# Gate and up products of a pair of experts, issued alternately for the one and the other expert

## Chip, cores and metric

The kernel runs on one core of a Trainium2 chip. The metric is device time in microseconds (us) of one execution, the median of several runs. Lower is better.

## What is computed

Two transformer blocks on 256 tokens of width 1024, all in fp32. The second ends with a mixture of experts: 32 experts in 4 groups, two of them per token, each expert a gated feed-forward layer of hidden width 512. Cut to what matters here (the routing gives `expert`, `weights` and the blocks of tokens per expert):

```python
def hier_moe(h, w_rg, b_rg, w_re, b_re, w_gate, w_up, w_down):
    ...
    def run_block(args):
        e, tok, w = args
        xb = xt[tok]
        hid = jax.nn.silu(xb @ w_gate[e]) * (xb @ w_up[e])
        return (hid @ w_down[e]) * w[:, None].astype(xb.dtype)
    ...
x = x + hier_moe(rmsnorm_2(x, g_moe[l]), ...)
return rmsnorm_2(x, g_final)
```

An expert's weights are 1024x512 (gate), 1024x512 (up) and 512x1024 (down) fp32 numbers, 2 MiB each, so all 32 experts have 192 MiB that must come from HBM.

## The kernel before

Everything up to the experts (both mixers, the first block's feed-forward layer, the cross attention) comes first and takes about 640 us; the change does not touch it. Then `moe` (lines 2045 to 2247) takes the experts two at a time. A pair `p` has experts `2p` and `2p+1`, here called `j = 0` and `j = 1`. Each expert has 64 places for tokens (`CAP`), so the two together fill 128 partitions: `H[0]` is partitions 0 to 63 and `H[1]` is 64 to 127. A product of one expert uses 64 columns of TensorE's array and writes 64 partitions of a PSUM bank; the other expert uses the other 64.

One turn of the loop over pairs issues, in this order:

- `gather` (every second turn, for two pairs): the tokens of the next experts, as columns, into `xe` (32 matmuls of 128x256).
- `hid_T`: four transposes of pair `p`'s hidden values (`sg`), copied to `hdT` by ScalarE.
- `gate_up(p+1)` (line 2097): gate and up products of the next pair. `k` runs over 8 slices of the width 1024, `c` is 0 for gate and 1 for up; `g[c]` is one PSUM bank for each. That is 8 x 2 x 2 = 32 products of 64x512. In the trace each fp32 product is two MATMUL instructions, so 64. After the first eight products (the first unit of weights of each expert, `k` 0 and 1) it calls `between`: `combine` (8 matmuls that add the pair before to the result) and `slots_T` (2 transposes). Then come the other 24 products.
- `down(p)` (line 2121): 4 slices x 2 halves `c` x 2 experts = 16 products of 64x512 (32 instructions). Here `j` already runs innermost.

After the last pair come `combine`, the final norm and the output (`norm_first`, `norm_out`).

The weights come in units of 1 MiB. A unit of `gate_up` holds the gate and the up rows of one expert for two values of `k` and is fetched as two transfers of 512 KiB; a unit of `down` is one transfer of 1 MiB (the last two units come as halves). `Experts.order` (line 349) lists them: 8 units for gate and up of pair 0, then for each pair the 8 units of the next pair's gate and up followed by the 4 units of its own down, the two experts' units alternating. All transfers are issued on SyncE's queue (SP), into 22 buffers in turn (`slots`: 4, then 5, then 13); a transfer waits until TensorE's last read of the unit that was in the buffer 22 units earlier. So TensorE has a store of up to 22 units, nearly two pairs, ahead of it.

TensorE issues its instructions in program order of `mm`, and the change moves only those of `gate_up`:

Of the kernel before, what the change touches and what calls it, by code (L numbers as in the profile page):

```python
# [421 lines left out]
class K:  # L422
# [1622 lines left out]
    def moe(self, A):  # L2045
# [51 lines left out]
        def gate_up(n, j0, ws_, between=None):  # L2097

            g = [self.bank() for _ in range(2)]
            for k, j, c in [(2 * q + i, j, c) for q in range(4) for j in range(n) for i in range(2) for c in range(2)]:  # L2100
                if between and (k, j, c) == (2, 0, 0):
                    between()
                self.mm(g[c][H[j]], xe[:, k, j0 + j], ws_(j, k // 2)[:, c, k % 2], k == 0, k == 7)
            sg = self.sg
            R = slice(0, n * CAP)
            nc.scalar.activation(sg[R], g[0][R], AF.Silu)
            V.tensor_tensor(sg[R], g[1][R], sg[R], op=ALU.mult)
            return sg
# [76 lines left out]
        quad = lambda p: rk[:, :, 2 * p:min(2 * p + 4, NE)]  # L2185
        gather(2, self.oh, [x])
        hd = gate_up(2, 0, unit(0))
        for t in range(2):
            nc.scalar.activation(xh[t], x[t], AF.Copy, scale=self.r[:, t:t + 1])
# [7 lines left out]
        for p in range(NP):  # L2197
            n = min(4, NE - 2 * (p + 1))
            if p % 2 == 0 and n:
                gather(n, oh, [xh, xl])  # L2200
            hdT = hid_T(2, hd)
            pw = one_hot(2, col(rk, p), col(W32, p))
            if p % 2 and p + 2 < NP:
                oh = hot(quad(p + 2), min(4, NE - 2 * (p + 2)))

            def between():
                nonlocal pT
                if p:
                    combine(pT)
                pT = slots_T(2, pw)  # L2210
            if n:
                hd = gate_up(2, 2 * (p % 2), unit(p + 1), between)
                X.load(12 * p + 16 + NR)
            else:
                final_gain()
                between()
                keep(NLAST)
            down(2, hdT, unit(p))
            X.load(12 * p + 20 + NR)
# [5 lines left out]
        with tc.If(most > CAP):  # L2225
            with tc.For_i(0, NE, 1) as e:
                one = bass.ds(e, 1)
                rke = A.tile([128, 2, 2], F32, name="rke")
                V.tensor_copy(rke[:, 0, :, None], rk[:, :, one])
                V.tensor_copy(rke[:, 1, :, None], W32[:, :, one])  # L2230
                wu = [X.fetch(spare[q], one, q) for q in range(6)]
                rk_, w_ = (lambda t, j: rke[:, 0, t:t + 1]), (lambda t, j: rke[:, 1, t:t + 1])
                for _ in range(1, T // CAP):
                    V.tensor_scalar(rke[:, 0], rke[:, 0], -float(CAP), None, op0=ALU.add)
                    gather(1, hot(rke[:, 0, :, None], 1), [xh, xl])
                    pT = slots_T(1, one_hot(1, rk_, w_))
                    down(1, hid_T(1, gate_up(1, 0, lambda j, q: wu[q])), lambda j, q: wu[q])
                    for c in range(2):
                        for t in range(2):
                            b = self.bank()  # L2240
                            for i in range(2):
                                self.mm(b, pT[H[0], t * 128:(t + 1) * 128], ys[c][i][H[0]], i == 0, i == 1)
                            sum_ = spare[7 + c][:, t * 512:(t + 1) * 512]
                            nc.scalar.activation(sum_, acc[t][c], AF.Copy)
                            V.tensor_tensor(acc[t][c], b, sum_, op=ALU.add)
            norm_first()
            norm_out()
# [27 lines left out]
```

## Time and profile before

| | |
|---|---|
| median of 3 runs | 1132.79 us (1130.45 to 1132.81) |
| profiled execution | 1131.38 us |
| its span, first to last instruction | 1129.6 us |
| TensorE matmul busy (PE) | 1107.8 us, 98% |
| TensorE weight load busy (PEld) | 784.5 us, 69% |
| VectorE, ScalarE, GpSimd busy | 45%, 34%, 5% |
| chain of work that ended last | 93% on PE |
| read from HBM | 297.83 MB |

The span begins at 0 and ends with the last instruction; all times in the rows below are from its start. "Busy" of PE is the time in which at least one matmul was under way, so two matmuls side by side in the two halves of the array count once. A view of stretches gives for each engine the busy time and, in brackets, the instructions; then the granted clock of TensorE as a share of 2.4 GHz, the share of time in which the DMA engines were busy, and GB/s.

### The profile page before, as it was taken

Reading aid. Unit: us, or ns where it says so; the run is one execution under the profiler, and the core shown is the slowest. Engines: PE = TensorE matmul, PEld = TensorE weight load, DVE = VectorE, ACT = ScalarE, POOL = GpSimd, SP = SyncE. Lnnn points to the kernel's source line nnn. Section 1 sums busy time; section 2 is a strip of 40 time slices with the busy share of each in tenths; the row PEclk is TensorE's granted clock in tenths of the full one; section 3 lists DMA queues with packets and bytes.
Section 4 is the critical chain, followed back from the end, with each engine's and each line's share of the span. In section 5 each row is a group of like instructions: output and inputs, shape, how many; then the busy total and the mean of one; then the engine's idle time right before and its main releaser. Section 6 shows DMA issues by size and latency. Waiting matters only on the chain.

```text
span 1129.6 us, 16831 instructions
## 1 busy us (share of the span) xinstructions
PE 1107.8 (98%) x6850; PEld 784.5 (69%) x6850; DVE 504.1 (45%) x917; ACT 381.2 (34%) x678; POOL 57.3 (5%) x85
## 2 busy tenths in 40 slices
PE   9999999999999999999999989999999999999996
PEld 8989788999999887989988644444444445444453
DVE  5777756656556576665666321212121212111112
ACT  6553556544344475565454210000000000000103
POOL 0153011000000010100000000000000000000000
PEclk9999999999999999999999999999999999999999
DMA  8454216674664544545498689999999999999931
GB/s 299 136 165 133 76 38 199 254 246 167 197 189 162 172 150 152 179 126 180 161 359 335 243 337 407 411 413 411 413 412 413 413 413 414 413 413 413 415 156 40
DMA packets 105950, 300.06 MB, mean 266 GB/s; under 512 B 6999, under 2 KB 35980, under 8 KB 97932
## 3 DMA queue, kind: packets, MB, share of 16 engines
q1 hardware_dynamic: 104700, 295.23, 69.6%
q0 software_dynamic: 1024, 3.17, 1.0%
q8 instruction: 56, 0.92, 0.3%
q10 hardware_dynamic: 144, 0.52, 0.1%
q14 instruction: 26, 0.21, 0.1%
HBM read 297.83 MB, written 1.07 MB: 265 GB/s over the span
## 4 chain that ended last, share of the span: by engine, by line
PE 93%; DVE 3%; ACT 2%; issue 1%; DMA 0%; POOL 0%; SPq 0%; ACTq 0%; DVEq 0%
PE bank L249 93%; ACT junk L249 1%; DVE cy L249 0%; DMA x<-in_x 0%; DVE junk L249 0%; DVE xTl L249 0%; ACT wh L249 0%; DVE x L249 0%; DVE xl L249 0%; ACT xTh L249 0%; DVE wm L249 0%; ACT sg L249 0%; DVE dp L249 0%; POOL nr L249 0%; DVE smz L249 0%
## 5 line engine op out<-in xcount | busy, mean ns | idle before, releaser
L249 PE MATMUL bank<-wm,xe 128*64 128x512 f32 x1024 | 285.1, 598 | 0.0
L249 DVE TENSOR_TENSOR wl<-wr,wh 128x1024 fp32r<-128x1024 f32 (+1 forms) x175 | 211.0, 1222 | 134.2 <-ACT wh L249 130.8
L249 PE MATMUL bank<-xTh,wh 128*128 128x256 f32 x768 | 223.1, 291 | 0.0
L249 ACT ACTIVATE wh<-wr 128x1024 fp32r<-128x1024 f32 (+1 forms) x175 | 180.1, 1050 | 118.2 <-PE bank L249 104.6
L249 PE MATMUL bank<-xTl,wh 128*128 128x256 f32 x768 | 217.3, 283 | 0.8 <-DVE xTl L249 0.8
L249 PE MATMUL bank<-xTh,wl 128*128 128x256 f32 x768 | 217.1, 283 | 0.2 <-DVE wl L249 0.2
L249 PEld LDWEIGHTS bank<-wm,xe 128*64 128x64 f32 x1024 | 101.0, 136 | 160.3 <-issue 157.1
L249 PEld LDWEIGHTS bank<-xTh,wh 128*128 128x128 f32 x768 | 147.0, 191 | 4.6 <-issue 2.4
L249 PEld LDWEIGHTS bank<-xTl,wh 128*128 128x128 f32 x768 | 147.1, 192 | 2.3 <-DVE xTl L249 1.2
L249 PEld LDWEIGHTS bank<-xTh,wl 128*128 128x128 f32 x768 | 147.0, 191 | 0.4 <-DVE wl L249 0.4
L249 PE MATMUL bank<-wm,hdT 128*64 128x512 f32 x512 | 128.7, 595 | 0.0
L249 ACT ACTIVATE sg<-bank 128x512 f32<-128x512 f32 x20 | 11.9, 597 | 295.3 <-PE bank L249 295.2
L249 DVE TENSOR_TENSOR sg<-bank,sg 128x512 f32<-128x512 f32 x16 | 11.1, 691 | 191.7 <-PE bank L249 191.7
L249 PEld LDWEIGHTS bank<-wm,hdT 128*64 128x64 f32 x512 | 46.5, 137 | 65.9 <-issue 60.7
L249 DVE SCALAR_TENSOR_TENSOR ys<-bank,ws,ys 128x512 fp32r<-128x512 f32 x32 | 24.0, 751 | 98.8 <-ACT ys L249 96.9
L249 ACT ACTIVATE ys<-bank,ws 128x512 fp32r<-128x512 f32 x32 | 22.0, 688 | 106.1 <-PE bank L249 106.1
L249 DVE TENSOR_SCALAR pwT<-bank 128x256 fp32r<-128x256 f32 x16 | 6.8, 424 | 90.1 <-PE bank L249 90.1
L249 POOL TENSOR_TENSOR nr<-nr,mhalf 128x2 f32<-128x2 f32 (+1 forms) x9 | 6.0, 673 | 713.0 <-DVE nr L249 712.9
L249 PE MATMUL bank<-wl,fhh 128*128 128x512 f32 x88 | 35.2, 400 | 0.0
L249 PE MATMUL bank<-wh,fhh 128*128 128x512 f32 x88 | 34.8, 395 | 0.0
L249 PEld LDWEIGHTS bank<-ys,pwT 128*128 128x128 f32 x128 | 22.8, 188 | 17.2 <-issue 11.4
L249 PE MATMUL bank<-ys,pwT 128*128 128x512 f32 x128 | 34.3, 408 | 0.3 <-DVE ys L249 0.3
(386 smaller groups left out, 1477.0 us busy)
## 6 DMA issues: line engine op xcount, KB each, us to landing
wm<-in_w_exp_gate SPq DMA_DIRECT2D x128, 512.0 KB, 10.2
wm<-in_w_exp_up SPq DMA_DIRECT2D x128, 512.0 KB, 10.2
wm<-in_w_exp_down SPq DMA_DIRECT2D x62, 1024.0 KB, 12.6
wr<-in_w_in SPq DMA_DIRECT2D x33, 1024.0 KB, 5.2
wr<-in_w_gate_up SPq DMA_DIRECT2D x22, 1024.0 KB, 5.7
wr<-in_w_down SPq DMA_DIRECT2D x11, 1024.0 KB, 5.1
wr<-in_w_out SPq DMA_DIRECT2D x8, 1024.0 KB, 5.1
wr<-in_w_ckv SPq DMA_DIRECT2D x4, 1024.0 KB, 6.3
```

The lines of the kernel that those rows point to most:

```text
L249: r = f(*args, **kw)
```

## The change

The list of products in `gate_up` is written in another order. Before, `q` (the unit) is outermost, then the expert `j`, then the two slices of the unit, then gate and up. After, the slice `k` is outermost, then gate and up, and the expert innermost. The test for `between` is rewritten for the new order and fires at the same place, after the first eight products.

```diff
         def gate_up(n, j0, ws_, between=None):
 
             g = [self.bank() for _ in range(2)]
-            for k, j, c in [(2 * q + i, j, c) for q in range(4) for j in range(n) for i in range(2) for c in range(2)]:
-                if between and (k, j, c) == (2, 0, 0):
+            for k, c, j in [(k, c, j) for k in range(8) for c in range(2) for j in range(n)]:
+                if between and (k, c, j) == (2, 0, 0):
                     between()
                 self.mm(g[c][H[j]], xe[:, k, j0 + j], ws_(j, k // 2)[:, c, k % 2], k == 0, k == 7)
```

No instruction is added or removed, and the orders of VectorE, ScalarE, GpSimd and SP stay as they are. On TensorE the first place is the first eight products of a `gate_up`, ahead of `between`. A row is one product: the bank it writes (`bank0_74` gate, `bank2_76` up), the weights' buffer (`wm2_6220` of the first expert, `wm3_6221` of the second) and the DMA counters it waits for. Before:

```order
L249 MATMUL bank0_74<-wm2_6220,xe_69 64x512 [waits DMAHW5_49]
L249 MATMUL bank2_76<-wm2_6220,xe_69 64x512 [waits DMAHW6_49,DVE_49]
L249 MATMUL bank0_74<-wm2_6220,xe_69 64x512
L249 MATMUL bank2_76<-wm2_6220,xe_69 64x512
L249 MATMUL bank0_74<-wm3_6221,xe_69 64x512 [waits DMAHW7_49]
L249 MATMUL bank2_76<-wm3_6221,xe_69 64x512 [waits DMAHW0_49]
L249 MATMUL bank0_74<-wm3_6221,xe_69 64x512
L249 MATMUL bank2_76<-wm3_6221,xe_69 64x512
```

After, at the same place on TensorE:

```order
L249 MATMUL bank0_74<-wm2_6220,xe_69 64x512 [waits DMAHW5_49]
L249 MATMUL bank0_74<-wm3_6221,xe_69 64x512 [waits DMAHW7_49]
L249 MATMUL bank2_76<-wm2_6220,xe_69 64x512 [waits DMAHW6_49,DVE_49]
L249 MATMUL bank2_76<-wm3_6221,xe_69 64x512 [waits DMAHW0_49]
L249 MATMUL bank0_74<-wm2_6220,xe_69 64x512
L249 MATMUL bank0_74<-wm3_6221,xe_69 64x512
L249 MATMUL bank2_76<-wm2_6220,xe_69 64x512
L249 MATMUL bank2_76<-wm3_6221,xe_69 64x512
```

Before, four products of the first expert are followed by four of the second; after, every other product is of the other expert, and the second expert's unit is waited for at the second product instead of the fifth.

The second place is the end of a `gate_up` on TensorE, where `down` (the rows that read `hdT_70`) follows without a break. Before:

```order
L249 MATMUL bank7_81<-wm12_6230,xe_69 64x512
L249 MATMUL bank3_77<-wm8_6226,xe_69 64x512 [waits DMAHW7_49]
L249 MATMUL bank7_81<-wm8_6226,xe_69 64x512 [waits DMAHW0_49]
L249 MATMUL bank3_77<-wm8_6226,xe_69 64x512
L249 MATMUL bank7_81<-wm8_6226,xe_69 64x512
L249 MATMUL bank2_76<-wm9_6227,hdT_70 64x512 [waits DMAHW1_49,Activation_49]
L249 MATMUL bank2_76<-wm6_6224,hdT_70 64x512 [waits DMAHW2_49]
L249 MATMUL bank3_77<-wm9_6227,hdT_70 64x512 [waits Activation_49]
```

After, at the same place on TensorE:

```order
L249 MATMUL bank7_81<-wm8_6226,xe_69 64x512 [waits DMAHW0_49]
L249 MATMUL bank3_77<-wm12_6230,xe_69 64x512
L249 MATMUL bank3_77<-wm8_6226,xe_69 64x512
L249 MATMUL bank7_81<-wm12_6230,xe_69 64x512
L249 MATMUL bank7_81<-wm8_6226,xe_69 64x512
L249 MATMUL bank2_76<-wm9_6227,hdT_70 64x512 [waits DMAHW1_49,Activation_49]
L249 MATMUL bank2_76<-wm6_6224,hdT_70 64x512 [waits DMAHW2_49]
L249 MATMUL bank3_77<-wm9_6227,hdT_70 64x512 [waits Activation_49]
```

Before, the four products ahead of `down` all belong to the second expert (`wm8_6226`); after, they alternate. `down` keeps its order, and its third product writes the bank of gate (`bank3_77`), so it waits until ScalarE has read that bank.

## Rows read from the trace of the kernel before

**Rows 1.** Page, parts 1 and 2: PE's busy time; DMA share and GB/s in 40 slices.
```profile
PE 1107.8 (98%) x6850; PEld 784.5 (69%) x6850; DVE 504.1 (45%) x917; ACT 381.2 (34%) x678; POOL 57.3 (5%) x85
...
DMA  8454216674664544545498689999999999999931
GB/s 299 136 165 133 76 38 199 254 246 167 197 189 162 172 150 152 179 126 180 161 359 335 243 337 407 411 413 411 413 412 413 413 413 414 413 413 413 415 156 40
```

**Rows 2.** Timeline of PE, one pair: start us, us, engine line op out<-in xcount.
```profile
927.96 5.42 PE L249 MATMUL bank<-wm,xe 128*64 128x512 f32 x16
933.31 2.13 PE L249 MATMUL bank<-ys,pwT 128*128 128x512 f32 x8
...
935.58 11.23 PE L249 MATMUL bank<-wm,xe 128*64 128x512 f32 x45
946.22 0.64 PE L249 MATMUL bank<-wm,hdT 128*64 128x512 f32 x1
946.65 0.59 PE L249 MATMUL bank<-wm,xe 128*64 128x512 f32 x1
...
947.93 7.04 PE L249 MATMUL bank<-wm,hdT 128*64 128x512 f32 x30
```

**Rows 3.** Timeline of PEld (weight loads), the same pair's gate-and-up and down.
```profile
928.87 0.14 PEld L249 LDWEIGHTS bank<-wm,xe 128*64 128x64 f32 x1 [0.29 <-issue]
...
929.73 0.19 PEld L249 LDWEIGHTS bank<-wm,xe 128*64 128x64 f32 x3 [0.29 <-issue]
...
948.37 0.18 PEld L249 LDWEIGHTS bank<-wm,hdT 128*64 128x64 f32 x2 [0.25 <-issue]
...
952.23 0.18 PEld L249 LDWEIGHTS bank<-wm,hdT 128*64 128x64 f32 x2 [0.25 <-issue]
```

**Rows 4.** Busy time by stretch: first gate-and-up; last pair to the end.
```profile
640.56:656.63 16.07, 16.06 (x65) 6.03 (x64) 0.69 (x1) 0.83 (x2) 0.00 (x0) 1.00 0.76 281
1104.54:1129.60 25.06, 14.87 (x73) 8.01 (x72) 7.77 (x16) 7.95 (x16) 1.12 (x2) 0.89 0.13 45
```

**Rows 5.** Busy time by stretch: the weights' stream, its steady part and its end.
```profile
681.00:1080.00 399.00, 399.00 (x1710) 180.56 (x1708) 74.31 (x157) 35.45 (x56) 0.00 (x0) 1.00 1.02 413
...
1084.00:1086.00 2.00, 2.00 (x9) 1.16 (x8) 0.66 (x2) 0.00 (x0) 0.00 (x0) 1.00 0.21 84
1086.00:1090.00 4.00, 4.00 (x17) 1.57 (x17) 0.09 (x1) 0.00 (x0) 0.00 (x0) 1.00 0.00 0
```

**Rows 6.** Page, part 6: sizes of the experts' transfers.
```profile
wm<-in_w_exp_gate SPq DMA_DIRECT2D x128, 512.0 KB, 10.2
...
wm<-in_w_exp_down SPq DMA_DIRECT2D x62, 1024.0 KB, 12.6
```

**Rows 7.** Timeline of PE: the last pair's transposes and down products.
```profile
1104.54 0.74 PE L249 MATMUL bank<-cst,sg 128*128 128x128 f32 x4
...
1109.94 7.09 PE L249 MATMUL bank<-wm,hdT 128*64 128x512 f32 x32
```

**Rows 8.** Busy time by stretch: the stream's stall after the first pair.
```profile
666.00:671.00 5.00, 5.00 (x16) 1.64 (x16) 1.11 (x5) 0.60 (x1) 0.00 (x0) 1.00 0.11 20
671.00:676.00 5.00, 5.00 (x19) 1.91 (x20) 0.76 (x2) 0.00 (x0) 0.00 (x0) 1.00 0.95 390
676.00:681.00 5.00, 5.00 (x26) 2.04 (x24) 0.00 (x0) 0.00 (x0) 0.00 (x0) 1.00 0.97 353
```

**Rows 9.** Timeline of SP: its issues around that stall.
```profile
654.88 16.81 SPq L249 DMA_DIRECT2D wm<-in_w_exp_down  x4
674.45 0.33 SPq L249 DMA_DIRECT2D wm<-in_w_exp_gate  x1
```

**Rows 10.** Busy time by stretch: TensorE short of work, and the granted clock.
```profile
390.20:393.70 3.50, 1.91 (x17) 1.68 (x17) 1.57 (x4) 1.90 (x8) 0.00 (x0) 1.00 0.48 186
...
656.00:661.00 5.00, 2.03 (x7) 1.05 (x6) 3.68 (x4) 2.46 (x3) 0.00 (x0) 0.89 1.03 412
661.00:666.00 5.00, 5.00 (x34) 4.88 (x33) 2.54 (x4) 0.00 (x0) 0.00 (x0) 0.76 0.98 407
```

## The prediction

> **What bounds the kernel now.** I read the page first. PE is busy 98% of the span, and in slices 25 to 37 the DMA engines are busy too, 9 tenths, moving 407 to 415 GB/s [rows 1]. Two things are near their limit in the experts' stage, so the next question is which of them ends last. The view by stretches answers it: from 681 to 1080 us the weights' stream runs at 413 GB/s with a busy share of 1.02, between 1084 and 1086 it falls to 84, and after 1086 it moves nothing [rows 5]. I take 1085.7 for its last landing. TensorE starts the last pair's transposes only at 1104.54 and its down products end at 1109.94 + 7.09 = 1117.03 [rows 7]. So today TensorE ends some 31 us behind the stream, and the stream itself has almost no room left.
>
> How TensorE spends its time is seen in the timeline of one pair. The two experts use two halves of the array, and the halves can work side by side. In the down products, where the experts alternate, two weight loads start together every (952.23 - 948.37) / 9 = 0.429 us [rows 3]: one instruction of each half per 0.429 us, which I call a slot. The last pair's 32 down instructions are 16 slots, 6.86 us, and take 7.09 [rows 7], so a run costs 0.23 us beside its slots. In gate and up, single loads mark stretches in which one half works alone (928.87), and loads by twos and threes those in which both do (929.73) [rows 3].
>
> A rule of the Trainium skill bears on this. The timeline first: a down product starts at 946.22, ahead of a gate-or-up product at 946.65 that stands before it in the program [rows 2], so one half does run ahead of the other. "TensorE: Matmul & The Clock Gate", Part 3 ("What overlaps and what doesn't"), says that matmuls start and end strictly in program order. By that, the 64 instructions of a gate-and-up would now take nearly 64 slots, 27 us, and the order would be worth some 13 us a pair on TensorE; the rows give (933.31 - 927.96) + (946.22 - 935.58) = 16.0 us [rows 2], so the trace disagrees, and the sum goes by the rows: most of the pairing exists already, and only the ends of each run, where one half is done before the other, are to be had.
>
> **The change, part by part.** Nothing is added or removed; the moves are on TensorE alone.
> - *First eight products*, 16 instructions ahead of the combine: 5.35 us now (927.96 to 933.31) [rows 2]. Alternating they are 8 slots + 0.23 = 3.66. Saved: 1.7.
> - *The other 24 and the 32 down instructions behind them*: from 935.58 to 947.93 + 7.04 = 954.97, 19.39 us [rows 2]. Alternating throughout they are 48 + 32 = 80 instructions, 40 slots + 0.23 = 17.39. Saved: 2.0.
> - *First pair's gate-and-up*, alone: 64 instructions in 16.07 us [rows 4]; 32 slots + 0.23 = 13.96. Saved: 2.1.
> - Sum on TensorE: 15 pairs x 3.7 + 2.1 = 57.6 us.
> - *Waits*: the second expert's unit is now needed at the second product, not the fifth. While the stream is ahead this costs nothing. Behind TensorE's queue then stand that pair's combine and down products. Once the stream limits, a step of two units needs both units in either order, and 16 instructions follow the later one: no difference worth a number. Down's third product waits for ScalarE's read of gate's bank; in the new order gate's last products end two slots ahead of up's, and up's last products and down's first two cover that read. Were a slot lost there in each pair, it would take 15 x 0.429 = 6.4 us of TensorE's gain, and not yet any of the kernel's, as comes below.
>
> That sum cannot all arrive, because the stream is the next to be late. A pair's weights are 16 x 512 KiB + 4 x 1 MiB [rows 6] = 12.58 MB, at 413 GB/s 30.5 us. TensorE, busy without a break from about 661, takes (1104.54 - 661) / 15 = 29.6 us a pair [rows 7, 10], and would take 25.9. It uses up its lag, then waits for landings. Unhindered it would start the last pair's transposes at 1104.54 - 57.6 = 1046.9; the stream does not allow it. The last pair's four down units (4.19 MB, 10.2 us) are the last to land, so the units of the pair before it are complete at 1085.7 - 10.2 = 1075.5. On them follow 16 instructions, 3.66 us, and the last pair's transposes at 1079.2: 25.3 us earlier than now. From there to the end 25.06 us stay as they are [rows 4]. The last down products would start 5.4 us later, at 1084.6, and need the last half unit only for their last quarter, so the stream's very end is covered.
>
> The second term is when the stream starts to run full. It stalls from 666 to 681 us, moving 20, 390 and 353 GB/s; against 413 that is 4.8 + 0.3 + 0.7 = 5.8 us lost [rows 8]. SP waits there for TensorE to free buffers: four issues run from 654.88 to 671.4, the next comes at 674.45 [rows 9]. In the changed kernel the products it waits for come 2.1 us earlier and their run is 1.7 shorter, 3.8 together. But the first expert's buffer, free today after its block alone, is then free only with the other's, so the first waiting issue gains just 2.1. Everything behind it gains 3.8. I take 3.5, near the larger end since all but one issue have it; the bounds are 0 (the stream ramps up as slowly as now) and 5.8 (the whole stall goes).
>
> **Sum.** 25.3 + 3.5 = 28.8 us. Against the profiled execution: 1131.38 - 28.8 = 1102.6; the median of the runs shown is 1.4 higher, so **1104.0 us** on its scale. Bounds: 1132.8 - 25.3 = 1107.5 above and 1131.4 - 31.1 = 1100.3 below. TensorE gains 57.6 and the kernel half of it; half the gain per pair (28.8 / 15 = 1.9) would be enough.
>
> **Rivals.**
> 1. *The halves do not pair further*, and the order does nothing: 1132.8. Against it: the down products have this very order, two instructions a slot [rows 3]. A part of the pairing gives something between; 1 us a pair would give 1132.8 - 15 - 2 = 1116.
> 2. *The clock falls in the waits, and the kernel gets slower.* TensorE would wait 28.8 us in all, 30.5 - 25.9 = 4.6 a pair, so over the last six pairs. When it had 2.03 us of work in 5, from 656 to 661, the granted clock went to its lower level: 0.89 in that stretch, 0.76 in the next [rows 10]. At half clock a pair takes 51.8 us, 21.3 more than the stream. More than 28.8 / 21.3 = 1.4 pairs' worth of it and the kernel is slower than before; all six would give about 1104 + 128 = 1232. Against it: from 390 to 394 us TensorE worked 1.91 of 3.50 us and the clock stayed at 1.00 [rows 10], and the waits to come are shorter: a step of two units takes the stream 2.10 MB / 413 = 5.1 us and TensorE 3.66, a wait of 1.4.
> 3. *Weight loads come out of cover.* In rows 3 a load of 0.14 us starts with each instruction inside a 0.429 us slot, hidden. If two loads a slot stood outside, a slot would be 0.71, and the 48 slots of a pair 13.4 us longer than forecast, 9.7 longer than now; with the first pair's 6.9 the kernel would take about 1285. The same Part 3 of the Trainium skill's "TensorE: Matmul & The Clock Gate" says that a load overlaps running matmuls only if its row group differs, and here all use every row; the down products of this trace [rows 3] disagree.
> 4. *The stream quickens* when buffers come free sooner. Its best slice has 415 GB/s against 413 [rows 1]: 2 us, 1102.
>
> **How the numbers follow.** Forecast 0.84; rival 1: 0.04 for none and 0.05 for a part; rival 2: 0.04; rival 3: 0.01; rival 4: 0.02. The likeliest case gives 1104. The range takes its bounds, 1100.3 and 1107.5, below them rival 4 and the 1.4 us between profiled time and median, to 1097; above, one brief fall of the clock in the last pair's 12.5 us (some 6 us), to 1114. It leaves out 0.14 at most. About 0.2% (2.3 us) is what can be told from no change: faster 0.84 + 0.05 + 0.02 = 0.91, same 0.04, slower 0.05.
>
> **What would show it.** Right: the 16-instruction run takes about 3.7 us and 24 products with down 17.4 in an early pair; weight loads by twos all through gate and up; from about the tenth pair on PE waits for the gate and up transfers, some 29 us in total; the stream ends near 1082 and the last transposes come near 1076; the clock stays at 1.00. Wrong: early pairs still 29.6 us long (rival 1), or a granted clock below 1 after 890 us (rival 2), or a PE that never waits for a landing, in which case the stream was not the limit I take it for.

## The result, and the profile after

The changed kernel takes **1104.95 us** (median; 1104.07 to 1105.21) against 1132.80 (1130.45 to 1133.51) for the kernel before. The ratio is 0.9752, with a 95% interval of 0.974 to 0.9764: 27.9 us less. The forecast was 1104.0. The profiled execution took 1105.21 us, its span is 1103.4, which is 26.2 less than the 1129.6 of before.

The page of the changed kernel, parts 1, 2 and 4, answers to [rows 1]:

```profile
PE 1064.0 (96%) x6850; PEld 749.7 (68%) x6850; DVE 504.1 (46%) x917; ACT 381.2 (35%) x678; POOL 57.3 (5%) x85
...
PE   9999999999999999999999989999999998989896
...
DMA  8454215676546435463569788999999999999993
...
PE 73%; DMA 21%; DVE 3%; ACT 2%; issue 1%; POOL 0%; SPq 0%; ACTq 0%; DVEq 0%
```

The chain of work that ended last was 93% PE before; now a fifth of it, 21%, is DMA. The DMA engines are busy into the last slice but one, and TensorE, short of work in this stage only at the first pair before [rows 10], has slices with idle time near the end.

One early pair in the changed kernel, timeline of PE (start us, us, engine line op out<-in xcount), answers to [rows 2]:

```profile
737.99 0.74 PE L249 MATMUL bank<-cst,sg 128*128 128x128 f32 x4
738.66 3.65 PE L249 MATMUL bank<-wm,xe 128*64 128x512 f32 x16
742.24 2.13 PE L249 MATMUL bank<-ys,pwT 128*128 128x512 f32 x8
744.21 0.38 PE L249 MATMUL bank<-cst,oh 128*128 128x128 f32 x2
...
744.52 10.52 PE L249 MATMUL bank<-wm,xe 128*64 128x512 f32 x48
754.87 7.04 PE L249 MATMUL bank<-wm,hdT 128*64 128x512 f32 x32
```

The first eight products take 3.58 us to the combine (before 5.35), the other 24 with the down products 754.87 + 7.04 - 744.52 = 17.39 us (before 19.39). Gate-or-up and down products no longer mix at the border (48, then 32, where [rows 2] have 1 and 1 out of turn), which fits two halves that end together. The weight loads (PEld) of the same pair's gate and up, to set beside [rows 3]:

```profile
747.57 0.14 PEld L249 LDWEIGHTS bank<-wm,xe 128*64 128x64 f32 x2 [0.28 <-issue]
748.00 0.14 PEld L249 LDWEIGHTS bank<-wm,xe 128*64 128x64 f32 x2 [0.28 <-issue]
```

Two loads every 0.43 us, as the down products had them. Late in the stage the picture is another. This is the last pair but one, timeline of PE:

```profile
1068.23 1.02 PE L249 MATMUL bank<-wm,hdT 128*64 128x512 f32 x2
1069.47 3.65 PE L249 MATMUL bank<-wm,hdT 128*64 128x512 f32 x16 [0.22 <-DMA wm<-in_w_exp_down]
1074.44 3.65 PE L249 MATMUL bank<-wm,hdT 128*64 128x512 f32 x14 [1.32 <-DMA wm<-in_w_exp_down]
1078.02 0.74 PE L249 MATMUL bank<-cst,sg 128*128 128x128 f32 x4
```

TensorE stands still until a down unit lands, works 3.65 us, and goes on to the last pair's transposes, now at 1078.02 (before 1104.54 [rows 7]). In the chain of waits the same stretch is written as transfers:

```profile
1034.01 15.01 DMA wm<-in_w_exp_up
1049.08 10.18 DMA wm<-in_w_exp_up
1059.32 15.08 DMA wm<-in_w_exp_down
1074.44 15.25 PE bank L249 x74
```

From 1034 to 1074 the chain goes from transfer to transfer, each issued when the one named before it had landed, and only from the landing at 1074.44 on is TensorE the chain again. The view by stretches, with the columns of [rows 4], [rows 5], [rows 8] and [rows 10]:

```profile
656.00:661.00 5.00, 3.66 (x14) 3.20 (x15) 3.14 (x4) 0.48 (x1) 0.00 (x0) 0.63 1.03 410
661.00:666.00 5.00, 5.00 (x28) 4.36 (x28) 2.62 (x6) 0.60 (x1) 0.00 (x0) 0.68 1.02 423
666.00:671.00 5.00, 5.00 (x26) 1.68 (x24) 1.10 (x4) 0.00 (x0) 0.00 (x0) 1.00 0.31 67
671.00:676.00 5.00, 5.00 (x26) 1.59 (x24) 0.00 (x0) 0.00 (x0) 0.00 (x0) 1.00 1.00 416
...
890.00:1077.00 187.00, 169.26 (x769) 67.54 (x769) 31.30 (x67) 15.21 (x24) 0.00 (x0) 1.00 1.02 413
1078.02:1103.40 25.38, 14.89 (x73) 8.01 (x72) 7.77 (x16) 7.96 (x16) 1.12 (x2) 0.89 0.30 115
```

The stream runs at the same 413 GB/s as before and no faster. Its stall after the first pair has shrunk (67 and 416 GB/s where there were 20 and 390). The clock stays at 1.00 through the waits from 890 us on, but around 660 us it is lower, and for longer, than before: 0.63 and 0.68, where there were 0.89 and 0.76.

Around the first pair, timeline of PE, first a line of the kernel before, then lines of the changed kernel, the last of them from the timeline of SP:

```profile
665.33 0.65 PE L249 MATMUL bank<-cst,sg 128*128 128x128 f32 x4
```

```profile
640.67 13.95 PE L249 MATMUL bank<-wm,xe 128*64 128x512 f32 x64
...
664.56 0.65 PE L249 MATMUL bank<-cst,sg 128*128 128x128 f32 x4
...
671.92 0.33 SPq L249 DMA_DIRECT2D wm<-in_w_exp_gate  x1
```

The first gate-and-up ends at 654.62 (before 656.62), the first pair's transposes come 0.8 us earlier, and SP's first issue for the next pair's gate 2.5 us earlier (before 674.45 [rows 9]).

### The profile page after: what moved, and what is told of

Read it like the earlier page. It is cut to its first block, busy times and chain, and to the rows that moved or that the text cites. A ratio compares the mean times of both kernels' runs of the same rounds, so it can differ in the third digit from the quotient of the medians.

```text
span 1103.4 us, 16790 instructions
## 1 busy us (share of the span) xinstructions
PE 1064.0 (96%) x6850; PEld 749.7 (68%) x6850; DVE 504.1 (46%) x917; ACT 381.2 (35%) x678; POOL 57.3 (5%) x85
## 4 chain that ended last, share of the span: by engine, by line
PE 73%; DMA 21%; DVE 3%; ACT 2%; issue 1%; POOL 0%; SPq 0%; ACTq 0%; DVEq 0%
PE bank L249 73%; DMA wm<-in_w_exp_up 15%; DMA wm<-in_w_exp_down 5%; ACT junk L249 1%; DVE cy L249 0%; DMA x<-in_x 0%; DVE junk L249 0%; DVE xTl L249 0%; ACT wh L249 0%; DVE x L249 0%; DVE xl L249 0%; ACT xTh L249 0%; DVE wm L249 0%; ACT sg L249 0%; DVE dp L249 0%
## 5 line engine op out<-in xcount | busy, mean ns | idle before, releaser
L249 PE MATMUL bank<-wm,xe 128*64 128x512 f32 x1024 | 230.7, 596 | 4.8 <-DMA wm<-in_w_exp_gate 4.3
L249 PEld LDWEIGHTS bank<-wm,xe 128*64 128x64 f32 x1024 | 71.1, 137 | 141.7 <-issue 122.5
L249 PE MATMUL bank<-wm,hdT 128*64 128x512 f32 x512 | 121.5, 595 | 12.9 <-DMA wm<-in_w_exp_down 12.9
L249 PEld LDWEIGHTS bank<-wm,hdT 128*64 128x64 f32 x512 | 37.9, 137 | 93.3 <-issue 67.5
L249 PE MATMUL bank<-ohr,xh 128*128 128x256 f32 (+1 forms) x128 | 34.3, 305 | 1.6 <-DVE ohr L249 1.6
L249 PE MATMUL bank<-ohr,xl 128*128 128x256 f32 (+1 forms) x128 | 33.9, 302 | 1.1 <-DVE xl L249 1.1
## 6 DMA issues: line engine op xcount, KB each, us to landing
wm<-in_w_exp_gate SPq DMA_DIRECT2D x128, 512.0 KB, 10.2
wm<-in_w_exp_up SPq DMA_DIRECT2D x128, 512.0 KB, 10.2
```

Of the source, the lines that this page charges most:

```text
L249: r = f(*args, **kw)
```

## The experiments

Two questions were open. Is it really the stream that halves the gain, or does the new order cost something elsewhere? And why does the stream start where it starts?

**The first eight products alone.** The kernel before, in which of each gate-and-up only the first eight alternate:

```diff
-            for k, j, c in [(2 * q + i, j, c) for q in range(4) for j in range(n) for i in range(2) for c in range(2)]:
+            turn = [(2 * q + i, j, c) for q in range(4) for j in range(n) for i in range(2) for c in range(2)]
+            pairs = [(k, j, c) for k in range(8) for c in range(2) for j in range(n)]
+            for k, j, c in pairs[:4 * n] + turn[4 * n:]:
```

> Only the first eight products of each gate-and-up alternate; the other 24 keep the old order. Theory (the slots of the prediction, with the stream as the limit): the 16-instruction run takes 3.65 us, the rest stays 19.3, TensorE gains 1.7 us in 15 pairs, 25.5 in all, just under what the stream allows, so the time is 1106 to 1108 us, although only half of the products were touched. Rival (the kernel keeps a fixed share, about half, of what TensorE saves, and the parts add up): 25.5 of 57.6 saved gives 12 of the 28 us, 1120.

Measured: 1106.08 us (1104.99 to 1108.49), ratio 0.9775 [0.9755, 0.9794]. In its trace the 16 instructions take 3.65 us and the rest starts as in the kernel before:

```profile
719.63 3.65 PE L249 MATMUL bank<-wm,xe 128*64 128x512 f32 x16
723.21 2.13 PE L249 MATMUL bank<-ys,pwT 128*128 128x512 f32 x8
...
725.49 11.23 PE L249 MATMUL bank<-wm,xe 128*64 128x512 f32 x45
736.13 0.64 PE L249 MATMUL bank<-wm,hdT 128*64 128x512 f32 x1
736.55 0.59 PE L249 MATMUL bank<-wm,xe 128*64 128x512 f32 x1
```

Eight of 32 products give 26.5 of the 28 us. The rival with its fixed share (1120) falls.

**The other 24 alone.** The mirror image: `turn[:4 * n] + pairs[4 * n:]` in the last line of the diff above.

> The first eight products keep the old order, the other 24 alternate. Theory: the run of 24 products and the down products behind them takes 17.4 us, the first run stays 5.35, TensorE gains 2.0 us in 15 pairs, 30 in all, a little more than the stream allows, so the time is 1104.5 to 1106.5, as with the whole change. Rival (the parts add up): 30 of 57.6 gives 15 of the 28 us, 1118.

Measured: 1108.13 us (1106.47 to 1109.06), ratio 0.9786 [0.9769, 0.9804]. The run of 24 products with down takes 17.39 us (736.77 + 7.04 - 726.42 in its timeline), the first run 5.42, as before [rows 2]; the rival's 1118 is far off. But the time is 1.6 us above the range that I gave. Two things account for it. With the first run in the old order the stream gains nothing at its start: its last transfer lands at 1085.3, as in the kernel before, and the last pair's transposes are at 1079.40, 1.4 later than in the changed kernel. And the clock fell once in the last pair, which it did not in the changed kernel's trace: the stretch from those transposes to the end is 26.4 us instead of 25.4.

```profile
1083.00:1086.50 3.50, 3.50 (x12) 2.24 (x12) 0.76 (x2) 0.00 (x0) 0.00 (x0) 0.52 0.30 123
```

So each part is worth 24 to 27 us alone (24.5 and 26.5 against 1132.59, the kernel before measured beside them) and both together 28. That is how a limit looks from the outside.

**Without the limit.** Both orders, with the down weights no longer transferred after the first 22 units:

```diff
         else:
...
-            nc.sync.dma_start(w, src)
+            if not isinstance(e, int) or self.n < 22:
+                nc.sync.dma_start(w, src)
         return w
...
-            for k in range(2):
-                for w, src in two:
-                    self.K.nc.sync.dma_start(w[:, k:k + 1], src[:, k:k + 1])
```

In the new order:

> The changed kernel without the transfers of the down weights after the first 22 units (the products read what lies in the buffers, so this part of the computation is left out). A pair then needs 8.4 MB, 20 us of the stream, and TensorE is the bound in both orders. Theory: the whole saving shows; pairs of 23.8 and 27.8 us to the end, 1074 to 1078 us. Rival (beside the stream's limit the alternating order costs something elsewhere, in waits for PSUM or for the other engines): over 1085.

In the old order:

> The kernel before without the same transfers. Theory: it was bound by TensorE, so leaving out a third of the stream changes nothing: 1130 to 1134 us, pairs of 27.5 and 31.6. Rival (the stream's traffic slows TensorE's reads, so the kernel before was bound by both): under 1125.

Measured: 1074.65 us in the new order, ratio 0.9491 [0.9472, 0.951]; 1133.63 (1131.56 to 1134.67) in the old, ratio 1.0011 [1.0001, 1.0022]. The new order, same stage, view by stretches and the last pair's transposes in the timeline:

```profile
681.00:1040.00 359.00, 359.00 (x1756) 152.07 (x1754) 74.40 (x158) 34.84 (x56) 0.00 (x0) 1.00 0.78 297
```

```profile
1047.57 0.74 PE L249 MATMUL bank<-cst,sg 128*128 128x128 f32 x4
```

Now PE is busy in every one of the 359 us, the DMA engines have room (0.78), and the last pair's transposes come at 1047.57: 57.0 us ahead of the kernel before, where the slots gave 57.6. Of that 0.7 is there at the first pair's transposes already (664.62 against 665.33), so the 15 pairs give 56.3. In the complete kernel they come at 1078.02, so the stream holds TensorE back by 30.5 us. Only 17.7 of them show as idle time (187.00 - 169.26 from 890 to 1077). The other 12.7 count as busy: from 661 to the last transposes PE is busy 399.28 us in the complete kernel and 386.57 here. Two down products ahead of a wait, at 1068.23 above, take 1.02 us where a slot is 0.43. In the old order a third less traffic in this stage changes nothing: there TensorE was the bound, and the stream did not slow it.

**The start of the stream.** The changed kernel with the split of `x` for the gathers ahead of the first gate-and-up:

```diff
         gather(2, self.oh, [x])
-        hd = gate_up(2, 0, unit(0))
         for t in range(2):
             nc.scalar.activation(xh[t], x[t], AF.Copy, scale=self.r[:, t:t + 1])
...
         for t in range(2):
             V.scalar_tensor_tensor(xl[t], x[t], self.r[:, t:t + 1], xh[t].bitcast(F32), op0=ALU.mult, op1=ALU.subtract)
+        hd = gate_up(2, 0, unit(0))
```

> The changed kernel, with the split of x (xh, xl) and the first selection matrix for the gather issued ahead of the first gate-and-up instead of behind it, so that TensorE does not stand still between that and the gather of the first pair, and the clock does not fall there. Theory (the stream sets the end, and its start is held by TensorE's freeing of buffers): the first pair's transposes come near 658.4 instead of 664.6, the clock stays at 1.00, the stall of the stream from 666 to 671 us shrinks by 3.6 us, the stream ends 3.6 earlier: 1101 to 1102 us. Rival (the stream is held by something else there): its end does not move, 1105.

Measured: 1102.78 us (1100.96 to 1103.49), ratio 0.9735 [0.9719, 0.9752]. The first pair's transposes are at 658.54, and the stall is gone:

```profile
656.00:661.00 5.00, 5.00 (x37) 3.74 (x37) 3.50 (x8) 0.60 (x1) 0.00 (x0) 1.00 1.04 415
661.00:666.00 5.00, 5.00 (x26) 1.60 (x24) 0.76 (x2) 0.00 (x0) 0.00 (x0) 1.00 1.02 420
666.00:671.00 5.00, 5.00 (x26) 1.73 (x24) 0.00 (x0) 0.00 (x0) 0.00 (x0) 1.00 1.00 418
671.00:676.00 5.00, 5.00 (x26) 1.60 (x23) 0.69 (x1) 0.60 (x1) 0.00 (x0) 1.00 1.02 408
1076.00:1079.00 3.00, 3.00 (x18) 2.60 (x17) 1.22 (x5) 1.26 (x3) 0.00 (x0) 0.82 0.66 266
1079.00:1081.00 2.00, 2.00 (x7) 1.50 (x7) 0.00 (x0) 0.00 (x0) 0.00 (x0) 0.50 0.17 70
```

The last pair's transposes come at 1074.69, 3.3 us earlier than in the changed kernel, where the theory had 3.6; the clock stays at 1.00 where it fell. The median is 0.8 us above the range that I gave. In the profiled execution the last rows say why: the clock fell at 1078, late, and the last stretch took 26.2 us instead of 25.4. The edit takes away TensorE's idle time and the fall of the clock together, so it does not say which of them held the stream by how much.

The same edit in the kernel before:

> The kernel before with the early split of e5. Theory (TensorE is the bound there, so all of it counts): the first pair's transposes come 4 to 6.5 us earlier, and the end as much: 1126.5 to 1129 us; in the changed kernel the same edit is worth only what the stream gains, 3.6. Rival (the stall is of no consequence to TensorE): 1132.

Measured: 1127.02 us (1126.34 to 1128.18), ratio 0.9954 [0.9936, 0.9972], 6.4 less than the 1133.39 of the kernel before measured beside it. Of that, 4.3 us show in the profiled executions: the first pair's transposes come at 660.97 (before 665.33), and the span is 1125.3 (before 1129.6). The other 2 lie between the profiled execution and the median of the kernel before. So in the kernel that TensorE bounds, what the first pair gains arrives whole at the end. In the one that the stream bounds, the first pair's transposes come 6.0 us earlier (658.54 against 664.56) and the last ones 3.3, of which 2.2 are left in the median (1104.95 to 1102.78).

**A version ahead of both.** As above, and `final_gain` moved from the last pair to the last but one, into TensorE's waits:

```diff
             else:
-                final_gain()
                 between()
                 keep(NLAST)
+            if p == NP - 2:
+                final_gain()
             down(2, hdT, unit(p))
```

> As e5, and the eight matmuls of final_gain stand ahead of the down products of the last pair but one, where TensorE waits for landings, instead of behind them. Theory: the way from that pair's last landing to the end becomes 1.3 to 2.0 us shorter, 1099 to 1100.5 us, faster than both kernels. Rival (the combine then waits for the evacuation of the down products that final_gain covered, and gives the gain back): as e5, 1101 to 1102.

Measured: **1099.59 us** (1098.87 to 1100.07), ratio 0.971 [0.9696, 0.9725]. Its last pair, timeline of PE:

```profile
1065.15 2.04 PE L249 MATMUL bank<-g,cst 8*128 8x128 f32 x16
1067.13 7.61 PE L249 MATMUL bank<-wm,hdT 128*64 128x512 f32 x32
1074.67 0.74 PE L249 MATMUL bank<-cst,sg 128*128 128x128 f32 x4
1075.17 2.18 PE L249 MATMUL bank<-ys,pwT 128*128 128x512 f32 x8
```

The 2.04 us of `final_gain` lie where TensorE would have waited, and the transposes come no later (1074.67 against 1074.69). The combine follows them at once, so the rival's wait for the evacuation did not appear. From the transposes to the end it is 1098.1 - 1074.67 = 23.4 us, where it was 25.4 in the changed kernel and 26.2 with the early split alone. So of the 2.8 us between these last two runs only 2.0 are `final_gain`'s; the other 0.8 is the fall of the clock, which did not come here.

**How far one half can run ahead.** The kernel before, with 12 products of one expert and then 12 of the other behind the first eight:

```diff
-            for k, j, c in [(2 * q + i, j, c) for q in range(4) for j in range(n) for i in range(2) for c in range(2)]:
+            turn = [(2 * q + i, j, c) for q in range(4) for j in range(n) for i in range(2) for c in range(2)]
+            pairs = [(k, j, c) for k in range(8) for c in range(2) for j in range(n)]
+            for k, j, c in turn[:4 * n] + [(2 + 2 * q + i, j, c) for q in range(0, 3, 3) for j in range(n) for i in range(6) for c in range(2)]:
```

> The kernel before with longer runs of one expert: after the first eight products, 12 of the first expert, then 12 of the second. It measures how far one half of the array can run ahead of the other. In the trace of before the second expert's first instruction starts with the fifth of the first's eight, so the reach seems to be four matmul instructions. Theory (a reach of four): the second expert starts with the 21st of the first's 24 instructions, 8.6 us after the run's start; the run and the down products take 25.7 us instead of 19.4, and the time is 1220 to 1240 us. Rival 1 (a deep reach): the halves overlap as before, 1133. Rival 2 (strict order, what was read as overlap being something else): 4 slots more a pair, 1160.

Measured once: 1238.05 us. The run starts at 929.87 in this pair. Weight loads, then matmuls:

```profile
938.07 0.14 PEld L249 LDWEIGHTS bank<-wm,xe 128*64 128x64 f32 x1 [0.29 <-issue]
938.50 0.19 PEld L249 LDWEIGHTS bank<-wm,xe 128*64 128x64 f32 x3 [0.29 <-issue]
938.93 0.19 PEld L249 LDWEIGHTS bank<-wm,xe 128*64 128x64 f32 x2 [0.24 <-issue]
...
939.85 0.14 PEld L249 LDWEIGHTS bank<-wm,xe 128*64 128x64 f32 x1 [0.29 <-issue]
```

```profile
929.87 17.87 PE L249 MATMUL bank<-wm,xe 128*64 128x512 f32 x45
947.15 0.64 PE L249 MATMUL bank<-wm,hdT 128*64 128x512 f32 x1
...
948.85 7.04 PE L249 MATMUL bank<-wm,hdT 128*64 128x512 f32 x30
```

Single loads until 938.07, then three at 938.50: the second expert starts 8.63 us after the run's start, 20 slots, with the first expert's 21st instruction. Run and down take 948.85 + 7.04 - 929.87 = 26.0 us. The theory of a reach of four had 8.6 and 25.7. With a deep reach the second expert would have started at once (1133). In strict order it would have started behind all 24, after 24 slots, 10.3 us, so the trace speaks against that too. The 1160 that I gave for strict order does not follow from it: four slots a pair more than with a reach of four would be some 1264 (an estimate: 1238 + 15 x 4 x 0.429).

## Why the prediction was right, point by point

- *What bounds the kernel.* Right. TensorE was the end and the stream close behind. The light kernels show it from both sides: without a third of the traffic the old order does not change (1133.63), and the new one drops to 1074.65.
- *TensorE's saving, 57.6 us.* Shown: 57.0 where nothing else limits. The first eight products 3.65 us (3.66 forecast), the other run 17.39 (17.39). The first pair's gate-and-up takes 13.95 us in the changed trace (13.96), but of its 2.1 us only 0.7 reaches the light kernel's first transposes; the 15 pairs gave 56.3 where 55.5 was forecast.
- *The stream as the limit, 25.3 us.* Right to 0.1: the last pair's transposes come 26.5 us earlier, of which the stream's earlier start, next point, is 1.3. Two small errors cancel in it: the last landing is at 1085.3 in the kernel before, not 1085.7, and in the changed kernel the last four units land 9.5 us behind the pair before (1083.9 - 1074.44), not 10.2. The last stretch takes 25.4 us instead of the 25.06 that were to stay.
- *The stream's earlier start, 3.5 us.* This is the term that was mis-sized: the stream's last transfer lands 1.3 us earlier (its stall, counted as in the prediction, went from 5.8 to 4.2 us). The first step that failed is that the products SP waits for "come 2.1 us earlier". They come 0.8 earlier: the first pair's transposes stand at 664.56, before at 665.33. The first gate-and-up did end 2.0 us sooner, but TensorE then waits for the selection matrix and the split of `x` nearly as long as before (2.72 us, before 2.96), and the clock, which fell once in that place before, now stays at its lower level until 664, twice as long. The row was in front of me ([rows 10], 0.89 and 0.76) and I used it for a rival only, not for this term. The second is the weighting, "near the larger end since all but one issue have it". SP's next issue for gate does come 2.5 us earlier, but by stretches of 1 us the stream is back above 400 GB/s from 671 on, where it was from 672 on before: 1 us, near what the first waiting issue gained. That this first issue sets the restart is read from these times and was not tested alone. The run with the early split takes the whole stall away; there the stream comes 3.3 us earlier than in the changed kernel. (Two readings were off without entering the sum: the four issues of [rows 9] end at 671.69, not 671.4, and the 415 GB/s of [rows 1] stand in slice 38.)
- *The same number nevertheless.* By spans the kernel gained 26.2 us and not 28.8. By medians it gained 27.9, because the profiled execution was 1.4 us under its median before and is 0.3 over it now. The prediction had taken those 1.4 us over to the changed kernel, and they were not there. Without that the forecast would have been 1102.6, further off: that 1104.0 lies so near to 1104.95 is in part luck.
- *The rivals.* None came. The halves pair fully. The clock does not fall in the waits for the stream: from 890 to 1077 us TensorE is busy 169 of 187 us and the clock is 1.00. Weight loads stay inside the slots, two per 0.43 us. The stream keeps its 413 GB/s.
- *What would show it.* The waits begin in the ninth turn (pairs of 27.8 and 23.8 us until 869, then 25.2 and 35.6), where I had said about the tenth. PE stands idle for 17.7 us, where I had said some 29; it is the whole delay against the light kernel that comes to 30.5. The stream ends at 1083.9 and the last transposes come at 1078.02, where I had said 1082 and 1076: both late by the mis-sized term.

## What to carry to other kernels

When two resources are both nearly busy, ask by how much the second would end earlier than the first. That lag, here 31 us, less the work that must still follow the second's last pieces, bounds what a change to the first alone can give: here 25 us, and a little more since the second started earlier. Part of the change may already give it: alternating 8 of 32 products gave 26.5 of 27.9 us. Where an array is shared by two halves, count how many instructions lie between the two halves' next ones; the loss sits at the ends of runs, and long runs of one half make it grow. And an idle stretch ahead of a stage is worth looking at together with the clock behind it, since the work there is paid at the lower level.

## What the runs showed of the hardware that was not expected

- The two 64-column halves of the array start out of program order, by a few matmul instructions and no more: with runs of 8 instructions of one expert the other starts beside the fifth (929.73 against 927.96, four slots [rows 2, 3]), with runs of 24 beside the 21st (938.50 against 929.87, 20 slots), both times beside the fourth from the end. Why it is four was not looked for.
- The granted clock can fall while TensorE is busy without a break. In the run with the early split it went to 0.82 and 0.50 at 1078 us, in a stretch in which PE was busy 3.00 of 3.00 us; just before it TensorE had done four transposes and 16 matmuls of 8 rows, and 3.6 us before the transposes a wait of 1.32 us had ended. The wait is not needed for it: in the light kernel in the old order PE was busy 442.50 of 442.50 us up to 1104, and behind the same transposes and matmuls the clock fell too:

```profile
1107.50:1110.90 3.40, 3.40 (x11) 2.58 (x11) 0.00 (x0) 0.60 (x1) 0.00 (x0) 0.57 0.00 0
```

  The changed kernel has the same instructions there, and its clock stayed at 1.00. What decides was not settled; the price in the run with the early split was about 0.8 us (26.2 against 25.4 for the last stretch).
